# A second seven-product pair in the first FFN phase, the order of the high halves behind a late pair, and other PSUM banks behind a pair

## Chip, cores and metric

The kernel runs on one core of a Trainium2 chip. The metric is the device time of one execution in microseconds, the median over runs; lower is better. Weights start in HBM and are streamed through SBUF during the run.

## What is computed

A trunk of two layers over 256 tokens of width 1024. Each layer is a half-step SwiGLU FFN, a mixer (differential attention on four heads beside mLSTM on four heads), and a second half-step FFN, each between RMS norms:

```python
def _swiglu(h, w_in, w_out):
    gate, up = jnp.split(h @ w_in, 2, axis=-1)        # w_in 1024 x 5632, so 2816 hidden units
    return (jax.nn.silu(gate) * up) @ w_out           # w_out 2816 x 1024

for l in range(DEPTH):                                # DEPTH = 2
    g = norm_gains[l]
    h = _swiglu(_rmsnorm(x, g[0]), ffn_w_in[l, 0], ffn_w_out[l, 0])
    x = x + 0.5 * _rmsnorm(h, g[1])
    h = _mixer(_rmsnorm(x, g[2]), mix_w_in[l], mix_w_out[l], ...)
    x = x + _rmsnorm(h, g[3])
    h = _swiglu(_rmsnorm(x, g[4]), ffn_w_in[l, 1], ffn_w_out[l, 1])
    x = x + 0.5 * _rmsnorm(h, g[5])
```

The change touches the FFN phases alone. There are six phases: 0 FFN, 1 mixer, 2 FFN, 3 FFN, 4 mixer, 5 FFN.

## The kernel before, in words

**Splitting.** Every float32 operand is used as a high half (a copy rounded to fp32r, made by ScalarE) and a low half (the difference, made by VectorE), and every product is three matmuls: high by high, high by low, low by high (`mm3`, L507 to L509). A weight piece is 128 x 2048 float32, 1 MB, brought by one DMA that SyncE issues (`fetch`, L289) into one of three `wr` buffers or, each fourth time in an FFN, the `wx` buffer. `halved` splits each half of a piece: ScalarE writes `wh` (L296), VectorE writes `wl` (L297). Seven `wl`/`wh` pairs exist, and of every ten halves three are lent buffers of another pool (`k4`), by a counter that runs through all phases.

**An FFN phase.** The 2816 hidden units are eleven chunks of 256. An ordinary chunk takes two pieces of `w_in` and runs 48 matmuls of 128 x 512 (two token tiles t, two halves kh of the width, four k, three matmuls) into two PSUM banks, one for each t; then Silu on ScalarE, the product with `up` on VectorE, and a turn of the hidden values by DMA: `ffn_planes` (ScalarE copy into two 16-bit planes, L646, and a DMA transpose on SyncE's queue, L648), `ffn_joined` (ScalarE puts the planes together again, L654), `ffn_split`/`ffn_hilo` (high half on ScalarE, L670; low half on VectorE, L671). The output product of a chunk (`out_part`, step O) is 24 matmuls into four `bk` banks that accumulate over all chunks.

**A pair.** A step P computes two chunks at once as a 2 x 2 block product with seven instead of eight block products (Winograd's form): `pair` runs seven times twelve matmuls (`product`, L756) into banks b1, b2 (`pin`) and b3, b4 (`ptr`), 84 where two ordinary chunks take 96. For this the four weight blocks are added in `pair_blocks` (eight VectorE operations of 128 x 1024, L323) and split as seven operands (fourteen halves, where two chunks have eight), and the token blocks in `pair_tokens` (steps S). The banks are evacuated by L770 to L793; the two token tiles are sent to be turned as they are ready, tile 0 first (`h0`), then tile 1 (`v`).

**The order of work.** `ONE` lists the steps of phase 0 and `TWO` those of phases 2, 3 and 5: I an ordinary chunk, L the weight piece of an output product, O an output product, S and P as above. `ONE` has one pair (chunks 7 and 8), `TWO` has two (4, 5 and 8, 9). The last chunk, 10, is computed transposed (`in_turned`, L731 and L736). At the end the output products of the chunks in `END` (8, 9, 10) run first for tile 0, then for tile 1. A planner of the framework decides, when the program is built, in which order each engine gets its instructions, from its own estimates; TensorE alone follows the written order from "ending" to the end of an FFN, through a following mixer, and until "running" of the next FFN. On the chip each engine takes its instructions in the order set.

**Banks.** Two banks `pin`, two `ptr`, four `bk`. Ordinary chunks in the step list take two `ptr`, then two `pin`, by turns (`swap`, which a pair leaves alone). Chunk 3 before the first pair of `TWO` uses `pin`, and chunk 6 behind it `ptr`.

**Late pairs.** `pair_ready` joins both tiles of a pair and then splits: join t0, join t1, then the high and low halves of chunk c (t0, t1) and of chunk c + 1 (t0, t1). It runs in the I step behind the pair, for the pair (8, 9) behind the pieces of chunk 10.

Of the kernel before, what the change touches and what calls it, by code (L numbers as in the profile page):

```python
# [28 lines left out]
NT = S // P  # L29
# [4 lines left out]
CH = P  # L34
EPS = 1e-6
BIG = -1.0e30
ONE = "I2 L1 S0 O0 I3 L2 S1 O1 I4 L3 S2 O2 I5 L4 O3 I6 L5 O4 P7 L6 O5 L7 O6 I9 L8 O7 I10 L9".split()
TWO = "I2 L1 S0 O0 I3 L2 S1 O1 S2 P4 L3 O2 L4 O3 I6 L5 O4 I7 L6 O5 P8 L7 O6 L8 O7 I10 L9".split()
END = (8, 9, 10)
AHEAD = 2  # L40
AT = (0, 2, 6, 6, 9, 22, 24, 24, 26, 26, 36, 40, 30, 46, 34, 50, 46, 52, 52, 57, 61, 60, 61, 67, 67, 69, 71, 78, 74, 74, 80, 84)
# [19 lines left out]
def _pack(inp):  # L61


    f32 = np.float32
    x = np.asarray(inp["x"])
    w_in, w_out = np.asarray(inp["ffn_w_in"]), np.asarray(inp["ffn_w_out"])
    m_in, m_out = np.asarray(inp["mix_w_in"]), np.asarray(inp["mix_w_out"])
    g = np.asarray(inp["norm_gains"])
    w = np.empty((L * PIECES_LAYER, P, 2048), f32)

    def ffn(at, l, f):
        n = w_in[l, f].reshape(2, 4, P, 2, NC_FF, 256).transpose(0, 3, 2, 1, 4, 5)
        a = n.transpose(4, 0, 2, 3, 1, 5).reshape(NC_FF, 2, P, 2048)
        b = w_out[l, f].reshape(NC_FF, 2, P, D).transpose(0, 2, 1, 3).reshape(NC_FF, P, 2048)
        order = [a[0, 0], a[0, 1], a[1, 0], a[1, 1], b[0]]
        for step in TWO if l or f else ONE:
            c = int(step[1:])
            if step[0] == "P":
                order += [n[kh, g, :, :, c:c + 2].reshape(P, 2048) for kh, g in ((0, 0), (0, 1), (1, 1), (1, 0))]
            elif step[0] in "IL":  # L80
                order += [a[c, 0], a[c, 1]] if step[0] == "I" else [b[c]]
        for piece in order + [b[END[-1]]]:
            w[at] = piece
            at += 1

    for l in range(L):
        at = l * PIECES_LAYER
        ffn(at, l, 0)
        at += PIECES_FFN
        for n, lo in enumerate(MIX_GROUPS):  # L90
            a = m_in[l][:, lo:lo + 512].reshape(2, 4, P, 512).transpose(0, 2, 1, 3)
            w[at + 2 * n:at + 2 * n + 2] = a.reshape(2, P, 2048)
        at += 2 * len(MIX_GROUPS)
        w[at:at + 4] = m_out[l].reshape(4, 2, P, D).transpose(0, 2, 1, 3).reshape(4, P, 2048)
        ffn(at + 4, l, 1)
    for i in range(2):
        w[i] = w[i].reshape(P, 4, 512).transpose(1, 0, 2).reshape(P, 2048)

    arrays = {
        "x": x.reshape(NT, P, 2, 512).transpose(0, 2, 1, 3),  # L100
        "w": w,
        "gpost": g[:, 1::2].reshape(L * 3, D),
        "lam": np.asarray(inp["da_lambda"]).reshape(L, 256),
    }
    arrays = {k: np.ascontiguousarray(v) for k, v in arrays.items()}
    gpre = g[:, 0::2].reshape(L, 3, KT, P).transpose(3, 0, 1, 2).reshape(P, L * 3 * KT)
    arrays["c0"] = np.concatenate([np.eye(P, dtype=f32), gpre], 1)

    inv = (f32(10000.0) ** (-np.arange(0, 64, 2, dtype=f32) / f32(64))).astype(f32)
    ang = np.arange(S, dtype=f32)[:, None] * inv[None, :]  # L110
    cos, sin = np.cos(ang).astype(f32), np.sin(ang).astype(f32)
    rope = np.stack([np.concatenate([cos, cos], 1), np.concatenate([-sin, sin], 1)])
    s = np.arange(P)[:, None]
    j = np.arange(P)[None, :]
    mask = np.where((s // CH == j // CH) & (s <= j), 0.0, BIG).astype(f32)
    first = (np.arange(S) % CH == 0)
    scan = np.stack([np.where(first, 0.0, 1.0), np.where(first, BIG, 0.0)]).astype(f32)

    def everywhere(v):
        return np.broadcast_to(np.asarray(v).reshape(1, -1), (P, np.asarray(v).size))  # L120

    parts = {
        "wg": m_in[:, :, 3072:3080].reshape(L, KT, P, 8).transpose(2, 0, 1, 3),
        "rope": rope.reshape(2, NT, P, 64).transpose(2, 0, 1, 3),
        "convw": np.asarray(inp["ml_conv_w"]).reshape(L, 4, 4, P).transpose(3, 0, 2, 1),
        "convb": np.asarray(inp["ml_conv_b"]).reshape(L, 4, P).transpose(2, 0, 1),
        "gda": np.asarray(inp["da_subln_g"]).T,
        "gml": np.asarray(inp["ml_norm_g"]).T,
        "gateb": everywhere(inp["ml_gate_b"]),
    }  # L130
    arrays["c1"] = np.concatenate([parts[n].reshape(P, -1) for n, _ in C1], 1)
    arrays["mask"] = mask
    arrays["scan"] = np.ascontiguousarray(np.broadcast_to(scan.reshape(1, 512), (100, 512)))
    return arrays


class _Trunk:
# [521 lines left out]
    def ffn_split(self, hs):  # L659

        ops = [self.ffn_operand() for _ in range(NT)]
        for h, op in zip(hs, ops):
            self.ffn_hilo(h, *op)
        return [[tuple(v[:, k] for v in op) for k in range(2)] for op in ops]

    def ffn_operand(self):
# [40 lines left out]
    def ffn(self, pre, gi_post):  # L707
# [3 lines left out]
        def in_piece(t, kh, pin, w):  # L711
            xh, xl = xT[t][kh]
            for k in range(4):
                self.mm3(pin, xh[:, k, :], xl[:, k, :], *self.cols(w, k),
                         start=kh == 0 and k == 0, stop=kh == 1 and k == 3)

        def out_part(c, t, h, wo):
            for hf in range(2):
                for k in range(2):
                    self.mm3(po[t][hf], *h[t][k], *self.cols(wo, 2 * k + hf),  # L720
                             start=c == 0 and k == 0, stop=c == NC_FF - 1 and k == 1)
# [20 lines left out]
        def ready(c, others):  # L742
            if c in sent:
                hT = self.ffn_joined(sent.pop(c), others)
                hs[c] = self.ffn_split([hT[:, t] for t in range(NT)])

        def chunk(c, pins):
            h = self.t2("h", (P, NT, 256))
            i = [self.ffn_hidden(pins[t], r[t], h[:, t]) for t in range(NT)]
            send(c, h)  # L750
            ready(c - 1, i[:1])
# [44 lines left out]

        def pair_ready(others):
            c, turned = sent.pop("pair")
            hT = [self.ffn_joined(v, others) for v in turned]
            for j in range(2):  # L800
                hs[c + j] = self.ffn_split([h[:, j] for h in hT])

        hs, po, wo, sent = {}, [], {}, {}
        kept = bool(xT)
# [21 lines left out]
        else:  # L826
# [6 lines left out]
            h = self.t2("h", (P, NT, 256))  # L833
# [13 lines left out]
            h = self.t2("h", (P, NT, 256))  # L847
# [5 lines left out]
            ready(0, [i])  # L853
        both, swap = list(self.both), 0
        tokens = self.pair_tokens(both, kept)
        steps = TWO if kept else ONE
        for at, step in enumerate(steps):
            kind, c = step[0], int(step[1:])
            if kind == "P":
                pair(c)  # L860
            elif kind == "S":
                sums = next(tokens)
            elif kind == "L":
                if wo.get(c) is None:
                    wo[c] = self.piece()
            elif kind == "I":
                if c == 3:
                    g = self.load_gpost(gi_post)
                    yield "middle"
                ws = [self.piece()]  # L870
                cut = self.cut
                ws.append(self.piece())
                if "pair" in sent and c != END[-1]:
                    pair_ready([cut])
                for later in steps[at + 1:]:
                    if later[0] != "L":
                        break
                    wo[int(later[1:])] = self.piece()
                if c == END[-1]:
                    if "pair" in sent:  # L880
                        pair_ready([self.cut])
                    ready(c - 1, [self.cut])
                    break
                pins = [self.bank_pin() if swap else self.bank_tr() for _ in range(NT)]
                swap = 1 - swap
                for kh in range(2):
                    for t in range(NT):
                        in_piece(t, kh, pins[t], ws[kh])
                chunk(c, pins)
            else:  # L890
                if not po:
                    po = [[self.bank_bk() for _ in range(2)] for _ in range(NT)]
                for t in range(NT):
                    out_part(c, t, hs[c], wo[c])
# [574 lines left out]
```

## Time and profile before

| | us |
|---|---|
| median of 3 runs | 947.07 (947.05 to 948.33) |
| the profiled execution | 949.07, of it the span 947.3 |
| phase 0 (from the start to about 183) | TensorE busy 180.94 of 183.00 |
| TensorE busy in the span | 936.2 (99%), 4439 matmuls |
| VectorE, ScalarE busy | 757.5 (80%), 664.5 (70%) |

Busy shares are averages; the chain of work that ended last and the waits of TensorE say where time can be saved. A matmul's end in the trace is modelled, so distances between matmuls are taken from start to start.

### The profile page before, as it was taken

What the parts mean: (1) busy time and instruction counts of PE and PEld (TensorE: products, weight loads), DVE (VectorE), ACT (ScalarE), POOL (GpSimd) and SP (SyncE); (2) the same over time, 40 slices, a digit from 0 to 9 for tenths busy, and PEclk for the clock granted to TensorE, in tenths of its full rate; (3) what the DMA queues carried; (4) which work ended last, traced back from release to release, by engine and by line L of the source; (5) the groups of instructions that cost most, each with busy time, mean ns of one, the idle gap of its engine ahead of it and who ended that gap; (6) DMA issues with size and microseconds to landing.
All of it is one profiled execution on the core that took longest, in us unless ns stands there. A gap on an engine that the chain in (4) does not pass through costs nothing.

```text
span 947.3 us, 12104 instructions
## 1 busy us (share of the span) xinstructions
PE 936.2 (99%) x4439; PEld 772.3 (82%) x4439; DVE 757.5 (80%) x1062; ACT 664.5 (70%) x1028; POOL 28.3 (3%) x57
## 2 busy tenths in 40 slices
PE   9999999999999999999999999999999999999997
PEld 6888888888788888788788888888888888888885
DVE  7966885789767989699698887968898587996983
ACT  7966767577765877676577766866779476776872
POOL 2000000000010000000000000000000100000000
PEclk9999999999999999999999999999999999999999
DMA  9995476336372766747557576573464449477631
GB/s 341 344 305 158 147 268 206 134 134 213 120 266 90 286 180 249 195 138 296 166 189 256 164 278 191 189 245 122 175 215 139 173 142 288 132 282 189 217 128 45
DMA packets 69882, 189.34 MB, mean 200 GB/s; under 512 B 45274, under 2 KB 46426, under 8 KB 49086
## 3 DMA queue, kind: packets, MB, share of 16 engines
q1 hardware_dynamic: 69246, 187.95, 59.3%
q8 instruction: 35, 0.57, 0.2%
q10 hardware_dynamic: 576, 0.61, 0.2%
q14 instruction: 25, 0.20, 0.1%
HBM read 177.01 MB, written 1.05 MB: 188 GB/s over the span
## 4 chain that ended last, share of the span: by engine, by line
PE 97%; DMA 1%; ACT 1%; DVE 0%; issue 0%; SPq 0%; POOLq 0%; DVEq 0%; ACTq 0%
PE pin L507 11%; PE pin L509 11%; PE pin L508 11%; PE bk L507 10%; PE bk L509 10%; PE bk L508 10%; PE ptr L756 8%; PE pin L756 6%; PE ptr L507 4%; PE ptr L509 3%; PE ptr L508 3%; PE pin L731 2%; PE ptr L731 1%; PE ptr L533 1%; PE ptr L1091 1%; PE pin L736 1%
## 5 line engine op out<-in xcount | busy, mean ns | idle before, releaser
L297 DVE TENSOR_TENSOR wl<-wr,wh 128x1024 fp32r<-128x1024 f32 x262 | 313.1, 1222 | 62.6 <-ACT wh L296 60.3
L296 ACT ACTIVATE wh<-wr 128x1024 fp32r<-128x1024 f32 x262 | 268.8, 1052 | 58.0 <-PE pin L509 12.3
L507 PE MATMUL pin<-wh,both 128*128 128x512 f32 x448 | 177.0, 398 | 0.0
L509 PE MATMUL pin<-wh,both 128*128 128x512 f32 x448 | 174.7, 390 | 0.0
L508 PE MATMUL pin<-wl,both 128*128 128x512 f32 x448 | 174.6, 390 | 0.0
L508 PE MATMUL bk<-wl,hh 128*128 128x512 f32 x352 | 137.0, 389 | 0.0
L507 PE MATMUL bk<-wh,hh 128*128 128x512 f32 x352 | 134.9, 391 | 1.7 <-ACT hh L670 1.7
L509 PE MATMUL bk<-wh,hl 128*128 128x512 f32 x352 | 133.1, 389 | 0.0
L509 PEld LDWEIGHTS pin<-wh,both 128*128 128x128 f32 x448 | 84.1, 188 | 18.0
L507 PEld LDWEIGHTS pin<-wh,both 128*128 128x128 f32 x448 | 84.3, 188 | 17.5 <-issue 0.7
L508 PEld LDWEIGHTS pin<-wl,both 128*128 128x128 f32 x448 | 84.2, 188 | 16.2
L296 ACT ACTIVATE wh<-wx 128x1024 fp32r<-128x1024 f32 x62 | 64.4, 1053 | 31.3 <-DMA wx<-in_w_dram 11.6
L297 DVE TENSOR_TENSOR wl<-wx,wh 128x1024 fp32r<-128x1024 f32 x62 | 75.4, 1222 | 10.4 <-ACT wh L296 10.4
L507 PEld LDWEIGHTS bk<-wh,hh 128*128 128x128 f32 x352 | 66.1, 188 | 15.7 <-ACT hh L670 2.3
L509 PEld LDWEIGHTS bk<-wh,hl 128*128 128x128 f32 x352 | 66.1, 188 | 14.1 <-DVE hl L671 0.4
L508 PEld LDWEIGHTS bk<-wl,hh 128*128 128x128 f32 x352 | 66.1, 188 | 13.5
L756 PE MATMUL ptr<-wh,both 128*128 128x512 f32 x224 | 73.3, 389 | 0.0
L507 PE MATMUL ptr<-wh,both 128*128 128x512 f32 x144 | 55.0, 391 | 0.9 <-DVE h L785 0.9
L508 PE MATMUL ptr<-wl,both 128*128 128x512 f32 x144 | 55.7, 389 | 0.0
L509 PE MATMUL ptr<-wh,both 128*128 128x512 f32 x144 | 55.7, 389 | 0.0
L756 PE MATMUL pin<-wh,both 128*128 128x512 f32 x168 | 55.1, 389 | 0.0
L654 ACT ACTIVATE hT<-h 128x1024 uint16<-128x1024 uint16 x33 | 45.0, 1364 | 6.2 <-DMA h<-planes 5.9
(261 smaller groups left out, 1418.6 us busy)
## 6 DMA issues: line engine op xcount, KB each, us to landing
wr<-in_w_dram SPq DMA_DIRECT2D x131, 1024.0 KB, 4.9
wx<-in_w_dram SPq DMA_DIRECT2D x31, 1024.0 KB, 4.9
gpost<-in_gpost_dram SPq DMA_DIRECT2D x6, 512.0 KB, 6.1
wr<-in_w_dram SPq DMA_DIRECT2D x2, 512.0 KB, 7.3
wr<-in_w_dram SPq DMA_DIRECT2D x3, 256.0 KB, 5.6
x<-in_x_dram SPq DMA_DIRECT2D x3, 256.0 KB, 6.1
h<-planes SPq DMA_TRANSPOSE x33, 4.1
out_dram<-x SPq DMA_DIRECT2D x2, 256.0 KB, 2.1
```

Source lines behind the costliest of these rows:

```text
L296: ia = nc.scalar.activation(hi, raw, AF.Copy)
L297: iv = nc.vector.tensor_tensor(lo, raw, hi.bitcast(F32), op=ALU.subtract)
L507: mm(ps, xh, wh, start=start, stop=False)
L508: mm(ps, xh, wl, start=False, stop=False)
L509: mm(ps, xl, wh, start=False, stop=stop)
L533: nc.tensor.transpose(ptr[:, k, :], x[:, (4 * hf + k) * P:(4 * hf + k + 1) * P], self.ident)
L654: i = self.nc.scalar.activation(hT.rearrange("p a b n -> p (a b n)").bitcast(U16).rearrange("p (n u) -> p u n", u=2), turned.rearrange("p ...
L731: self.nc.tensor.matmul(b, self.cols(w[kh], k)[0][:, c], both[kh][:, k].rearrange("p i t -> p (i t)"), start=kh == 0 and k == 0, stop=Fals ...
L736: self.nc.tensor.matmul(b[:, 0:NT * P], self.cols(w[kh], k)[1][:, c], both[kh][:, k, 0:NT].rearrange("p i t -> p (i t)"), start=False, sto ...
L756: self.nc.tensor.matmul(b, st[:, k, :], self.cols(w, k)[mv], start=new and k == n == 0, stop=k == 3 and n == 2, skip_group_check=True)
L1091: self.T(ptr[:, b, :], a[:, b * P:(b + 1) * P], self.tr.ident)
```

## The change

Four edits. (1) Phase 0 follows the same list as the others, with pairs (4, 5) and (8, 9) in place of the one pair (7, 8); the order of the packed weight pieces follows. (2) `pair_ready` makes the four operands first and then goes tile by tile: join t0, high and low halves of t0 for both chunks, join t1 behind the two high halves of t0, high and low halves of t1. (3) After a pair `swap` is 1, so that the next ordinary chunk takes `pin` banks and the one after it `ptr`. (4) `ffn_split` gets its last line from a helper.

```diff
-ONE = "I2 L1 S0 O0 I3 L2 S1 O1 I4 L3 S2 O2 I5 L4 O3 I6 L5 O4 P7 L6 O5 L7 O6 I9 L8 O7 I10 L9".split()
-TWO = "I2 L1 S0 O0 I3 L2 S1 O1 S2 P4 L3 O2 L4 O3 I6 L5 O4 I7 L6 O5 P8 L7 O6 L8 O7 I10 L9".split()
+STEPS = "I2 L1 S0 O0 I3 L2 S1 O1 S2 P4 L3 O2 L4 O3 I6 L5 O4 I7 L6 O5 P8 L7 O6 L8 O7 I10 L9".split()
...
-        for step in TWO if l or f else ONE:
+        for step in STEPS:
...
             self.ffn_hilo(h, *op)
+        return self.ffn_pairs(ops)
+
+    @staticmethod
+    def ffn_pairs(ops):
         return [[tuple(v[:, k] for v in op) for k in range(2)] for op in ops]
...
             c, turned = sent.pop("pair")
-            hT = [self.ffn_joined(v, others) for v in turned]
+            ops = [[self.ffn_operand() for _ in range(NT)] for _ in range(2)]
+            for t in range(NT):
+                h = self.ffn_joined(turned[t], others)
+                others = [self.ffn_hilo(h[:, j], *ops[j][t])[0] for j in range(2)]
             for j in range(2):
-                hs[c + j] = self.ffn_split([h[:, j] for h in hT])
+                hs[c + j] = self.ffn_pairs(ops[j])
...
             if kind == "P":
                 pair(c)
+                swap = 1
```

More of the change, by code (lines that the diff above doesn't have):

```diff
@@ L855, in ffn @@
         tokens = self.pair_tokens(both, kept)
-        steps = TWO if kept else ONE
-        for at, step in enumerate(steps):
+        for at, step in enumerate(STEPS):
             kind, c = step[0], int(step[1:])
@@ L874, in ffn @@
                     pair_ready([cut])
-                for later in steps[at + 1:]:
+                for later in STEPS[at + 1:]:
                     if later[0] != "L":
```

## The prediction

> **What bounds the kernel now.** I read the head of the page first, then the chain of work that ended last, then TensorE's own waits, and went to the timeline only where a wait stands.
>
> ```profile
> span 947.3 us, 12104 instructions
> PE 936.2 (99%) x4439; PEld 772.3 (82%) x4439; DVE 757.5 (80%) x1062; ACT 664.5 (70%) x1028; POOL 28.3 (3%) x57
> PE 97%; DMA 1%; ACT 1%; DVE 0%; issue 0%; SPq 0%; POOLq 0%; DVEq 0%; ACTq 0%
> ```
>
> The span, the busy times, and the engines' shares of the chain: TensorE is busy 99% of the span and carries 97% of the chain. A matmul's modelled end overlaps the next start, so "busy" can hide short gaps. What a matmul costs comes from distances between starts; these two lines of the chain, in the pair of phase 0, show it:
>
> ```profile
> 112.44 2.72 PE pin L756 x12
> 115.16 2.72 PE ptr L756 x12
> ```
>
> Twelve 512-column matmuls take 2.72 us, 0.227 us each, group behind group. TensorE's waits (us in total, times, longest; the two rows left out are, like the second, from the first 10 us), and phase 0 behind its start:
>
> ```profile
> PE bk L507 <- ACT hh L670: 1.7, 1, 1.7
> PE ptr L455 <- DMA x<-in_x_dram: 0.9, 1, 0.9
> PE ptr L507 <- DVE h L785: 0.9, 3, 0.6
> ...
> ```
>
> ```profile
> 10.00:183.00 173.00, 173.00 (x784) 1.00 0.70 238
> ```
>
> The second row is the input at the start. The other two lie in FFN phases: 1.7 us once for a high half, 0.9 us in three places for an evacuation (L785). From 10 to 183 us TensorE has no gap. So time falls where matmuls go away or where one of these two waits goes away, and rises where a new wait appears.
>
> **The change, part by part.** The sum is made against the profiled execution: 949.07 us, span 947.3, so 1.77 us lie around the span. The median of the runs, 947.07, is 2.0 us below that execution; I subtract the sum from the median, since what is removed is matmuls and waits inside the span.
>
> *Phase 0's second pair: matmuls.* Before, chunks 4, 5, 9 are ordinary and 7, 8 a pair; after, 4, 5 and 8, 9 are pairs and 7 is ordinary. One more pair: 96 matmuls become 84. Twelve at 0.227 us: **-2.72 us**, all on the path, since this stretch has no gap. The Trainium skill, "TensorE: Matmul & The Clock Gate", section "Back-to-back issue gap", gives about 131 ns for a 512-column matmul in a sustained stream and about 216 ns for an isolated one; twelve would be worth 1.57 or 2.59 us, estimates from that page, and the sum below 4.81 or 5.83 us in place of 5.96. The trace's 2.72 us decides.
>
> *Phase 0's second pair: the other engines.* The durations:
>
> ```profile
> L297 DVE TENSOR_TENSOR wl<-wr,wh 128x1024 fp32r<-128x1024 f32 x262 | 313.1, 1222 | 62.6 <-ACT wh L296 60.3 <-PE bk L509 1.7
> L296 ACT ACTIVATE wh<-wr 128x1024 fp32r<-128x1024 f32 x262 | 268.8, 1052 | 58.0 <-PE pin L509 12.3 <-PE bk L509 11.5 <-DMA wr<-in_w_dram 9.3
> L323 DVE TENSOR_TENSOR qk<-qk,wr 128x1024 f32<-128x1024 f32 x14 | 17.1, 1222 | 0.1
> L785 DVE TENSOR_TENSOR h<-ptr,u 128x512 f32<-128x512 f32 x7 | 4.8, 686 | 2.8 <-PE ptr L756 2.8
> L793 DVE SCALAR_TENSOR_TENSOR v<-v,rs,u 128x512 f32<-128x512 f32 x7 | 5.2, 747 | 0.0
> L638 DVE SCALAR_TENSOR_TENSOR h<-pin,rs,sil 128x256 f32<-128x256 f32 x32 | 15.3, 481 | 0.9 <-ACT sil L268 0.9
> ```
>
> VectorE gets six more splits and eight block additions, 14 x 1.222 = 17.1 us, and the pair's evacuation (five operations of 0.69, two of 0.75, 4.9 us) for that of two chunks (4 x 0.48 = 1.9): +20.1 us. ScalarE gets six casts, 6 x 1.052 = 6.3 us; its Silus, planes and joins about balance. DMA bytes stay the same: four block pieces for four chunk pieces, one transpose for each tile instead of each chunk. They move on SyncE's queue, and the two diagonal-sum blocks hold `wr` buffers until their last addition, so the pieces behind (L4, chunk 6) are fetched later. POOL has no step here. The added token sums (S2) are not new, only written earlier. Whether this is covered is read from the stages; phase 3, which already has both pairs, is the model for phase 0 after:
>
> ```profile
> 0.00:183.00 183.00, 180.94 (x813) 147.88 (x814) 136.25 (x188) 130.11 (x188) 6.65 (x22) 1.00 0.71 240
> 483.00:650.00 167.00, 166.84 (x757) 138.47 (x755) 139.41 (x167) 120.43 (x155) 1.55 (x5) 1.00 0.64 213
> 40.00:63.00 23.00, 23.00 (x103) 19.06 (x102) 18.47 (x26) 19.18 (x28) 0.00 (x0) 1.00 0.99 323
> ```
>
> Phase 0 would hold (136.3 + 20.1) / 180 = 87% on VectorE and (130.1 + 6.3) / 180 = 76% on ScalarE, against 83% and 72% in phase 3, whose TensorE is busy 166.84 of 167.00 us. On average it fits. The critical place is the early one: the third row shows DMA at 0.99 share from 40 to 63 us, just before the new pair. So the question is VectorE's lead:
>
> ```profile
> 48.78 0.42 DVE L221 TENSOR_REDUCE c_lams<-lamp 128x4 f32<-128x256 f32 x1
> 50.88 2.36 DVE L297 TENSOR_TENSOR wl<-wr,wh 128x1024 fp32r<-128x1024 f32 x2 [1.68 <-PE bk L509]
> 53.08 1.06 ACT L296 ACTIVATE wh<-wx 128x1024 fp32r<-128x1024 f32 x1 [0.51 <-DMA wx<-in_w_dram]
> 63.32 0.39 PE L507 MATMUL ptr<-wh,both 128*128 128x512 f32 x1
> ...
> 514.87 1.23 DVE L323 TENSOR_TENSOR qk<-wx,wr 128x1024 f32<-128x1024 f32 x1 [0.31 <-DMA wr<-in_w_dram]
> 532.92 0.39 PE L756 MATMUL pin<-wh,both 128*128 128x512 f32 x1
> 553.07 4.63 DVE L297 TENSOR_TENSOR wl<-wr,wh 128x1024 fp32r<-128x1024 f32 x4
> ```
>
> Phase 3 begins the pair's additions at 514.87 and its first product at 532.92, a lead of 18.0 us. In phase 0 the work behind chunk 3 begins where O1 ends, at 63.32 (now chunk 4, then the pair). VectorE has caught up by then: it is done at 49.2 with all splits of L2 and waits at 50.88 for TensorE to free a weight half, so the halves are full. Of the 14.1 us until 63.3 it needs about 1.7 for the hidden values of chunks 2 and 3; lead about 12.4 us. The third block (`wx`) has landed by 53.08, the fourth one piece later, about 3.3 us at 323 GB/s, so 56.4. The need: 22 operations at 1.135 us (four back to back took 4.63 us, so (4.63 - 1.22) / 3 from one to the next) make 25.0 us, with four evacuations 27.4, against 19.0 us for 84 matmuls: a deficit of 8.4, with the first cast and split 10.7 us. 12.4 covers it, and O2 and O3 (48 matmuls, 10.9 us) stand ready as filling. I take **0**; bounds: 0, and -2.72 given back whole (the pair starves as long as it saves).
>
> *Banks behind a pair.* Three stalls, each the last matmul of an output product and the first of chunk 6 (phases 2, 3, 5):
>
> ```profile
> 382.68 0.39 PE L509 MATMUL bk<-wh,hl 128*128 128x512 f32 x1
> 383.68 0.47 PE L507 MATMUL ptr<-wh,both 128*128 128x512 f32 x1 [0.61 <-DVE h L785]
> ...
> 562.62 0.39 PE L509 MATMUL bk<-wh,hl 128*128 128x512 f32 x1
> 563.16 0.47 PE L507 MATMUL ptr<-wh,both 128*128 128x512 f32 x1 [0.16 <-DVE h L785]
> ...
> 849.86 0.39 PE L509 MATMUL bk<-wh,hl 128*128 128x512 f32 x1
> 850.41 0.47 PE L507 MATMUL ptr<-wh,both 128*128 128x512 f32 x1 [0.16 <-DVE h L785]
> ```
>
> Start to start 1.00, 0.54 and 0.55 us; less 0.227 that makes 0.77 + 0.32 + 0.32 = **1.41 us** (the waits row says 0.9, by modelled ends). Chunk 6 waits for a `ptr` bank, freed by L785 behind the pair's last products. With `pin` it takes b1 and b2, last read by the Silu of b1 and by L774, both long before. What is late next are chunk 6's weights:
>
> ```profile
> 381.70 1.23 DVE L297 TENSOR_TENSOR wl<-wr,wh 128x1024 fp32r<-128x1024 f32 x1 [1.72 <-ACT wh L296]
> 382.85 0.68 DVE L785 TENSOR_TENSOR h<-ptr,u 128x512 f32<-128x512 f32 x1
> ```
>
> The second half of its first piece is split at 381.70 to 382.93; it is needed six matmuls in, 382.91 + 1.36 = 384.27 us if chunk 6 starts without the gap. Margin 1.3 us, so nothing replaces the wait. Chunk 7 then takes `ptr`, a whole chunk (10.9 us) after the pair. In the late pair P5 writes b4, which chunk 7's tile 1 leaves; O5 (5.4 us) and P1 (2.7 us) lie between, against two operations of 0.5 us. Bounds: 1.41 gained, or 0 if the planner's new order puts another wait there. I take 1.41. Phase 0 had no such stall and gets none.
>
> *High halves behind each join.* The tail of phase 2 on ScalarE, then TensorE:
>
> ```profile
> 456.06 1.37 ACT L654 ACTIVATE hT<-h 128x1024 uint16<-128x1024 uint16 x1 [2.10 <-DMA h<-planes]
> 457.46 0.42 ACT L670 ACTIVATE hh<-hT 128x256 fp32r<-128x256 f32 x1
> 460.37 1.35 ACT L654 ACTIVATE hT<-v 128x1024 uint16<-128x1024 uint16 x1 [1.94 <-DMA v<-planes]
> 461.58 0.39 ACT L268 ACTIVATE su<-su 128x256 f32<-128x256 f32 x1
> 461.88 1.01 ACT L670 ACTIVATE hh<-hT 128x256 fp32r<-128x256 f32 x3
> ...
> 460.58 0.39 PE L509 MATMUL bk<-wh,hl 128*128 128x512 f32 x1
> 462.64 0.50 PE L507 MATMUL bk<-wh,hh 128*128 128x512 f32 x1 [1.67 <-ACT hh L670]
> ```
>
> Join t0 (456.06) gives one high half, 457.46; the next joins wait: ScalarE idles 1.94 us for the transpose of `v`, joins t1 at 460.37, and the three other high halves follow from 461.88. TensorE, which needs chunk 9 of tile 0 next, stands from 460.58 to 462.64: 2.06 - 0.227 = **1.83 us**. After, both halves of t0 are cast by 458.2, before 460.58 + 0.227, and t1 is needed only after 8 and 9 and 10 of tile 0 (36 matmuls, 8.2 us from 457.93, so 466.1), while its join ends at 461.7. Next late is chunk 10 of tile 0, needed at 457.93 + 24 x 0.227 = 463.4: its Silu stands at 461.58 behind the join, then product, cast and low half, about 463.3. That is close; bounds 1.83 gained, or 1.3 if it is half a microsecond late. I take 1.83. In phases 3 and 5 and, after, 0, the halves come before they are needed, so nothing. The rest of the edit (operands made earlier, a new order of ScalarE instructions) adds no instruction.
>
> Sum: 2.72 + 1.41 + 1.83 = **5.96 us**, so 947.07 - 5.96 = **941.1 us** (943.1 for an execution like the profiled one).
>
> **The rivals.** *The pair in phase 0 pays for itself.* For it: DMA at 0.99 share and 20.1 us more on an engine that was saturated until 49 us; buffers held longer. Against it: the lead above. Price: the 2.72 come back, the waits still go: 943.8.
>
> *The waits only move.* The planner orders anew, and a moved matmul meets another bank, weight half or low half. For it: chunk 10's margin of a tenth; against it: the 1.3 us at chunk 6. Only the matmuls remain: 944.3.
>
> *TensorE is not the limit.* If the modelled 99% hides that VectorE (80%) or the weight loads set the pace, neither matmuls nor waits count and the time stays at 947.1. Against it: groups of twelve at a constant 2.72 us, which a limit elsewhere would break. The Trainium skill, "Perfetto Trace Analysis", section "Identifying the Most-Contended Engine", speaks for this rival: matmul busy time is a poor measure, and weight-load busy time is to be read, here 82%, hardly above VectorE's 80%. The trace bears it out only in so far as four short gaps hid in "busy".
>
> *Slower.* One mechanism: VectorE enters the early pair of phase 0 without lead, and the planner has put O2 and O3 behind the pair instead of into it. Then TensorE waits up to the 10.7 us above less the lead. It decides for slower by over 0.2% (1.89 us) when the stall is over 5.96 + 1.89 = 7.85 us, so when the lead is under 2.9 us. With no lead: 951.8. Against it stand 12.4 us expected and 18.0 us in phase 3.
>
> **How the numbers follow.** Runs of this kernel spread over 1.3 us, so 0.2% (1.9 us) is about what a measurement can tell from no change. Chances: the forecast 0.62 (its own range 940.2 to 942.6, up by the chunk-10 margin and a stall of a microsecond in the new pair, down by what the runs spread), the pair that pays for itself 0.14, waits that move 0.10, TensorE not the limit 0.08, slower 0.06. Faster ends at 945.2: the first three but 0.03 of them, 0.83; same 0.11; slower 0.06. The range 940.2 to 945.0 takes in the forecast, the second and most of the third, 0.82.
>
> **What the profile of the changed kernel would show.** L756 at 672 matmuls (588 before), L507 to L509 96 fewer, and a second early pair in phase 0 from about 63 us, with TensorE without gaps to the end of the phase. If the pair starves, TensorE waits there for `wl` (L297) or for L323. The L785 row is gone from TensorE's waits, and chunk 6 writes `pin`. In phase 2's tail two high halves follow the first join without a gap, the wait of `bk` for `hh` is under 0.3 us, and ScalarE still idles for `v` with nobody waiting. The prediction is wrong if a new wait of over a microsecond stands at phase 0's pair, at chunk 6 or at chunk 10's output product.

## The result, and the profile after

The changed kernel takes 942.35 us (median of 5 runs, 942.2 to 944.36) against 948.01 us (5 runs on the same chip, the three of above among them): ratio 0.9946, 95% interval 0.9933 to 0.9960, so 5.1 us faster (3.8 to 6.4), 5.66 by the medians. The forecast was 941.1 from 947.07, 5.96 less; with five runs the kernel before lies 0.94 us higher than the 947.07 that the forecast started from, so the time came out 1.25 us above 941.1, while the change is 0.3 us smaller than forecast by the medians and 0.9 by the ratio. The profiled execution of the changed kernel took 944.36 us. The head of its page, then its pair groups beside those of before (TensorE, matmuls of a shape with their count; line numbers are each kernel's own, here and below):

```profile
span 942.6 us, 12085 instructions
PE 933.1 (99%) x4427; PEld 770.2 (82%) x4427; DVE 776.2 (82%) x1079; ACT 668.5 (71%) x1033; POOL 29.5 (3%) x57
PE 94%; DMA 2%; DVE 2%; ACT 2%; issue 0%; SPq 0%; POOL 0%; POOLq 0%; DVEq 0%; ACTq 0%
```

```profile
L759 PE MATMUL ptr<-wh,both 128*128 128x512 f32 x256 | 84.0, 389 | 0.0
L759 PE MATMUL pin<-wh,both 128*128 128x512 f32 x192 | 63.0, 389 | 0.0
```

```profile
L756 PE MATMUL ptr<-wh,both 128*128 128x512 f32 x224 | 73.3, 389 | 0.0
L756 PE MATMUL pin<-wh,both 128*128 128x512 f32 x168 | 55.1, 389 | 0.0
```

TensorE has 12 matmuls fewer and 8 pairs in place of 7 (256 : 224 and 192 : 168 are 8 : 7). It is still busy 99%, while its share of the chain fell from 97% to 94%, and VectorE and ScalarE now carry 2% each. What that costs is read from TensorE's own waits, here complete:

```profile
PE ptr L532 <- DVE x L589: 0.8, 2, 0.4
PE ptr L454 <- DMA x<-in_x_dram: 0.8, 1, 0.8
PE bk L495 <- PEq L1465: 0.8, 1, 0.8
PE bk L482 <- ACT wh L472: 0.4, 1, 0.4
PE bk L508 <- DVE hl L674: 0.2, 1, 0.2
```

Both waits on which the forecast rested are gone (`hh` L670, now L673; L785, now L788). In their place stand two lines that were not there: transposes (L532) waiting for x from the post-norm, and a high-by-low product waiting for `hl`, the low half of hidden values. Phase 0 from 10 us on, its whole, and the stretch beside the new pair (each row: stretch and length, busy time and instructions of TensorE, its weight loads, VectorE, ScalarE and GpSimd, then granted clock, busy share of the DMA engines, GB/s):

```profile
10.00:180.00 170.00, 170.00 (x772) 141.39 (x770) 149.53 (x194) 129.43 (x181) 3.13 (x8) 1.00 0.72 241
0.00:180.00 180.00, 178.06 (x801) 145.54 (x802) 153.29 (x205) 134.91 (x193) 6.57 (x22) 1.00 0.73 244
63.00:92.00 29.00, 29.00 (x130) 24.01 (x129) 27.59 (x29) 23.71 (x28) 0.00 (x0) 1.00 0.55 197
```

TensorE has no gap in phase 0 up to its end at 180 us. VectorE rose from 136.25 to 153.29 us there, by 17.0 (20.1 forecast). Where the 4.7 us between the two spans (947.3 and 942.6) lie, from start to start: 2.72 in matmuls, 1.41 + 1.83 in the two waits that went, against 0.55 us in phase 2's tail and 0.26 + 0.56 + 0.56 at the ends of phases 0, 2 and 3; the rest, 0.7 us, is in the first 12 us and in gaps of about 0.2 us and less. None of the new waits is over a microsecond, and none stands at phase 0's pair or at chunk 6, which writes `pin` now.

### The profile page after: what moved, and what is told of

Its sections match the earlier page's. It is cut to its first block, busy times and chain, and to the rows that moved or that the text cites. A ratio compares the mean times of both kernels' runs of the same rounds, so it can differ in the third digit from the quotient of the medians.

```text
span 942.6 us, 12085 instructions
## 1 busy us (share of the span) xinstructions
PE 933.1 (99%) x4427; PEld 770.2 (82%) x4427; DVE 776.2 (82%) x1079; ACT 668.5 (71%) x1033; POOL 29.5 (3%) x57
## 4 chain that ended last, share of the span: by engine, by line
PE 94%; DMA 2%; DVE 2%; ACT 2%; issue 0%; SPq 0%; POOL 0%; POOLq 0%; DVEq 0%; ACTq 0%
PE pin L506 11%; PE pin L508 10%; PE pin L507 10%; PE bk L506 9%; PE bk L507 9%; PE bk L508 9%; PE ptr L759 9%; PE pin L759 7%; PE ptr L507 3%; PE ptr L508 3%; PE ptr L506 3%; PE ptr L734 1%; PE pin L734 1%; PE ptr L532 1%; DMA v<-planes 1%; PE ptr L1097 1%
## 5 line engine op out<-in xcount | busy, mean ns | idle before, releaser
L506 PE MATMUL pin<-wh,both 128*128 128x512 f32 x432 | 171.2, 399 | 0.0
L507 PE MATMUL pin<-wl,both 128*128 128x512 f32 x432 | 168.4, 390 | 0.0
L508 PE MATMUL pin<-wh,both 128*128 128x512 f32 x432 | 168.2, 390 | 0.0
L508 PEld LDWEIGHTS pin<-wh,both 128*128 128x128 f32 x432 | 81.1, 188 | 17.4
L506 PEld LDWEIGHTS pin<-wh,both 128*128 128x128 f32 x432 | 81.3, 188 | 17.1 <-issue 0.7
L507 PEld LDWEIGHTS pin<-wl,both 128*128 128x128 f32 x432 | 81.2, 188 | 15.5
L759 PE MATMUL ptr<-wh,both 128*128 128x512 f32 x256 | 84.0, 389 | 0.0
L296 DVE TENSOR_TENSOR wl<-wx,wh 128x1024 fp32r<-128x1024 f32 x62 | 74.7, 1219 | 10.1 <-ACT wh L295 9.3
L759 PE MATMUL pin<-wh,both 128*128 128x512 f32 x192 | 63.0, 389 | 0.0
L759 PEld LDWEIGHTS ptr<-wh,both 128*128 128x128 f32 x256 | 48.1, 188 | 10.0
L507 PE MATMUL ptr<-wl,both 128*128 128x512 f32 x128 | 49.8, 389 | 0.0
L508 PE MATMUL ptr<-wh,both 128*128 128x512 f32 x128 | 49.8, 389 | 0.0
L759 PE MATMUL ptr<-wl,both 128*128 128x512 f32 x128 | 49.8, 389 | 0.0
```

The lines of the kernel that those rows point to most:

```text
L296: iv = nc.vector.tensor_tensor(lo, raw, hi.bitcast(F32), op=ALU.subtract)
L506: mm(ps, xh, wh, start=start, stop=False)
L507: mm(ps, xh, wl, start=False, stop=False)
L508: mm(ps, xl, wh, start=False, stop=stop)
L759: self.nc.tensor.matmul(b, st[:, k, :], self.cols(w, k)[mv], start=new and k == n == 0, stop=k == 3 and n == 2, skip_group_check=True)
```

## The experiments

The kernels ran in three groups of four, each group on another chip together with the kernel before, so ratios to before are compared across groups, not microseconds. "Old count" means the count of lent halves as it stands before the change at phase 1; phase 0's second pair makes six more halves, so the list shifts it by six. The traces show what such a shift does. Behind phase 0 every engine has the same order of instructions in the kernel before and in e9_list_count, and again the same in e1_list and e11_count; between these two groups the order differs in every engine but GpSimd. Which halves lie in lent buffers shifts along with the order, and no run here separates the two.

| kernel | edit | ratio to before (95%) | us |
|---|---|---|---|
| e1_list | list alone (count shifted) | 0.9949 (0.9935 to 0.9964) | -4.8 |
| e2_banks | banks alone | 0.9979 (0.9967 to 0.9992) | -2.0 |
| e3_joins | joins alone | 0.9973 (0.9963 to 0.9984) | -2.6 |
| e4_fourth | changed kernel, fourth half behind the post-norm | 0.9915 (0.9902 to 0.9928) | -8.1 |
| e9_list_count | list alone, old count | 0.9967 (0.9955 to 0.9979) | -3.1 |
| e10_after_count | changed kernel, old count | 0.9928 (0.9911 to 0.9946) | -6.8 |
| e6_adds2 | changed kernel, 8 more VectorE operations | 1.0002 (0.9989 to 1.0014) | +0.2 |
| e7_adds3 | changed kernel, 16 more | 1.0106 (1.0085 to 1.0127) | +10.1 |
| e11_count | shifted count alone | 0.9961 (0.9949 to 0.9974) | -3.7 |
| e12_best | changed kernel, old count, fourth half | 0.9917 (0.9898 to 0.9935) | -7.9 |
| e13_list_fourth | list and fourth half | 0.9919 (0.9898 to 0.9941) | -7.7 |
| after_again | changed kernel | 0.9936 (0.9918 to 0.9954) | -6.1 |

**One part at a time.** The list alone is the first two hunks of the diff; the banks alone are `swap = 1`; the joins alone are the new `pair_ready`.

> The kernel before with phase 0 on the list of the other phases, and nothing else. Theory (the terms add): L756 at 672, twelve matmuls fewer, -2.72 us; the old banks leave chunk 6 of phase 0 a wait on L785 as in phases 3 and 5, +0.3 to +0.8; so -1.9 to -2.4 us against before, and no other wait in phase 0. Rival (the pair pays for itself): waits of 2 us or more for split weights in phase 0, time within 0.7 us of before. On the new waits at the phase ends (TensorE on L589, 0.26 + 0.56 + 0.56 us after the change): if the list brings them (a shifted count of lent halves), they stand here too, and the gain is 0.5 to 1.0; if the order of the joins brings them, there is none.

> The kernel before with swap = 1 behind a pair, and nothing else. Theory: the three waits of chunk 6 on L785 (0.77 + 0.32 + 0.32 us) go and nothing takes their place: -1.4 us in the trace, the wait of 1.8 us in phase 2's tail stays. Rival (waits only move): another wait of 0.3 us or more at chunk 6 or 7, or at a phase end, and the trace within 0.5 us of before.

> The kernel before with the high halves behind each join, and nothing else. Theory: the 1.83 us in phase 2's tail become about 0.5 (chunk 10's low half comes late), so -1.3 us there. If the new order of ScalarE at the tail is what lets the planner put a fourth cast of the next phase ahead of the post-norm's square, the waits on L589 stand here (up to 0.26 + 0.56 + 0.56), and the net is about 0; if not, -1.3 us net.

TensorE's waits of the three (without the start), first the list, then the banks, then the joins:

```profile
PE ptr L533 <- DVE x L590: 0.6, 2, 0.5
PE bk L507 <- ACT hh L670: 0.3, 1, 0.3
```

```profile
PE bk L507 <- ACT hh L670: 1.2, 1, 1.2
```

```profile
PE ptr L507 <- DVE h L785: 0.9, 3, 0.6
```

Banks and joins did what the forecast says: with the banks alone L785 is gone, with the joins alone the wait for `hh` is gone, and neither brings a wait at a phase end. (With the banks alone the wait for `hh` stands, 1.2 us.) By their runs they are worth 2.0 (0.8 to 3.1) and 2.6 us (1.5 to 3.5), forecast 1.41 and 1.83. The list alone surprised: 4.8 us where 1.9 to 2.4 was expected, with **no wait on L785 in any phase** though the banks were the old ones, 0.3 us left for `hh`, and the new waits at the phase ends. Why L785 stopped mattering is seen on TensorE's timeline around the end of phase 3's first pair, the last matmul of the pair and the first of chunk 6, before and with the list alone, with VectorE's L785 of the latter (start, length, instruction, and in brackets the idle time before it with what ended it):

```profile
561.03 0.39 PE L756 MATMUL ptr<-wh,both 128*128 128x512 f32 x1
563.16 0.47 PE L507 MATMUL ptr<-wh,both 128*128 128x512 f32 x1 [0.16 <-DVE h L785]
```

```profile
552.66 0.39 PE L756 MATMUL ptr<-wh,both 128*128 128x512 f32 x1
557.19 0.39 PE L507 MATMUL ptr<-wh,both 128*128 128x512 f32 x1
...
553.97 0.68 DVE L785 TENSOR_TENSOR h<-ptr,u 128x512 f32<-128x512 f32 x1
```

Before, 2.13 us and 7 output matmuls lie between the two; with the list alone 4.53 us and 19. The evacuation is done at 554.65, long before chunk 6 asks for the bank at 557.19. Phase 3's code was not touched: the planner ordered it anew, and more output products stand between the pair and chunk 6.

**Is it the shifted count?** Two kernels complete the square: the list with the count put back, and the count shifted without the list.

```diff
-            seen = 0
+            seen, self.halves = 0, self.halves + 4 * (ph == 1)   # e9, e10, e12: old count (six back, modulo ten)
+            seen, self.halves = 0, self.halves + 6 * (ph == 1)   # e11: shifted count, list of before
```

> The kernel before with phase 0 on the list of the other phases and the count of lent halves put back at phase 1, so that from the end of phase 0 every engine has the same order of instructions as in the kernel before. Theory (the pair is worth its matmuls; what the list alone brought beyond them comes from the shifted count): TensorE's waits on L785 (0.77 + 0.32 + 0.32) and the 1.8 us in phase 2's tail stand again, no wait on L589, and the time is 2.7 us under before. Rival (the list itself removes those waits): they stay away and the time is 5 to 6 us under before, as with the list alone.

> The kernel before, phase 0 untouched, with six added to the count of lent halves at phase 1; from there every engine has the order of instructions that it has with the list alone. Theory (the shifted count, by the order that the planner then makes, removes the waits): no wait on L785, under 1 us left in phase 2's tail, new waits of 0.3 to 0.6 us on L589 at two or three phase ends; 1.5 to 2.8 us under before. Rival (phase 0's pair is needed for it): the waits of before stand, time as before.

TensorE's waits behind the start, first list with old count, then shifted count alone:

```profile
PE bk L507 <- ACT hh L670: 2.5, 2, 1.7
PE ptr L507 <- DVE h L785: 0.9, 3, 0.6
PE ptr L533 <- DVE x L590: 0.4, 1, 0.4
```

```profile
PE ptr L533 <- DVE x L590: 0.2, 1, 0.2
```

The count carries it. With the old count everything behind phase 0 has the order of before, both waits stand again (the one for `hh` even longer, 2.5 us in two places of phase 2's tail), and the pair is worth 3.1 us (2.0 to 4.3) against 2.72 forecast. With the count alone, and not one instruction less, both waits are gone and 3.7 us (2.5 to 4.8) are gained, more than the 1.5 to 2.8 expected, with short waits at the phase ends (0.31, 0.28 and 0.29 us from start to start).

> The changed kernel with the count of lent halves put back at phase 1. Theory (the terms of the sum hold at the old count, and the waits at the phase ends come from the shifted count): no wait on L785, none of over 0.1 us on L589, 0 to 0.6 us left in phase 2's tail: 0.8 to 1.4 us under the changed kernel, 5.4 to 6.0 us under before. Rival (the waits at the phase ends come from the order of the joins or from the banks): 0.5 us each on L589 stay, time as the changed kernel.

With the old count the whole change gives 6.8 us (5.1 to 8.4), with waits of 0.3 us for `hh` and none on x behind the start: the three terms of the forecast hold together there (5.96). Against the changed kernel it is not clearly faster, since the intervals overlap; the waits at the phase ends are gone as expected, though.

**The waits at the phase ends.** At the end of phase 3 ScalarE casts halves of the next phase's first weights and then squares for the post-norm of tile 0; x is written by VectorE behind that, and the next phase's transposes need x. ScalarE before, after, and with the fourth half ordered behind the post-norm; then TensorE after:

```profile
643.13 2.94 ACT L296 ACTIVATE wh<-wr 128x1024 fp32r<-128x1024 f32 x3
645.98 0.58 ACT L577 ACTIVATE junk<-bk 128x512 bf16<-128x512 f32 x1
```

```profile
638.28 3.89 ACT L295 ACTIVATE wh<-wr 128x1024 fp32r<-128x1024 f32 x4
642.07 0.57 ACT L576 ACTIVATE junk<-bk 128x512 bf16<-128x512 f32 x1
```

```profile
635.60 2.94 ACT L295 ACTIVATE wh<-wr 128x1024 fp32r<-128x1024 f32 x3
638.45 0.57 ACT L576 ACTIVATE junk<-bk 128x512 bf16<-128x512 f32 x1
...
639.59 1.05 ACT L295 ACTIVATE wh<-wr 128x1024 fp32r<-128x1024 f32 x1
```

```profile
646.61 0.41 PE L532 MATMUL ptr<-c,x 128*128 128x128 f32 x2 [0.40 <-DVE x L589]
```

After the change a fourth cast of 1.0 us stands ahead of the square: 3.89 us for four where three took 2.94. x is written 0.5 us later against the 24 matmuls of tile 1 that cover it, and TensorE waits. Before, that chain had no margin either: the transposes started 0.30 us behind the last matmul of tile 1, which is 0.07 us more than the usual 0.23, and 0.25 us more were lost among them until the second half of x was written. With the order of before, the list with the old count shows a wait of 0.4 us there.

```diff
-            self.turns = [self.guards] * 4 + [last[:1], post] if ph else []
+            self.turns = [self.guards] * 3 + [first, last[:1], post] if ph else []   # first: post-norm of tile 0
```

> The changed kernel, with the fourth half of the next phase's first weights ordered behind the post-norm of token tile 0 (its cast behind the second square on ScalarE, its split behind the write of x on VectorE) instead of behind the last chunk's high half. Theory (the new waits at the phase ends come from a fourth cast of 1.05 us ahead of the square): TensorE's waits on L589 go or fall under 0.1 us each, -1.1 to -1.4 us against the changed kernel, so about 941.1. Rival (the post-norm's own chain, from the last matmul of tile 0 through square, power and x, is longer than the 24 matmuls of tile 1 that cover it): the waits stay at 0.5 us.

All waits on x went, and the wait for `hl` with them: the fastest kernel here, 940.39 us, 8.1 us under before (6.8 to 9.3). The interval lies clear of the changed kernel's in the first comparison (3.8 to 6.4) and overlaps that of its second, below (4.4 to 7.8): that the fourth half's place brings something is shown by the waits, its size (some 2 to 3 us) only roughly. From start to start its trace has lost the two gaps of phase 2's tail, the three at the phase ends and three of 0.25 us inside the transposes, 2.7 us together.

> The changed kernel with the old count and with the fourth half of the next phase's weights behind the post-norm of tile 0. Theory: with the old count only 0.5 us in phase 2's tail and three gaps of 0.2 us inside the transposes at the phase ends (L532 behind L532) are left to take; the ordered fourth half took those three away in its own run: 0.4 to 0.8 us under the changed kernel with the old count. Rival: nothing left to gain, 942.

> The list alone, with the fourth half behind the post-norm of tile 0, and neither the banks nor the joins. Theory (at the shifted count the banks and the joins have nothing left to remove): as the changed kernel with the fourth half in place, within 0.8 us. Rival (the banks and joins carry the forecast's 3.2 us): 2 to 3 us slower than that.

> The changed kernel once more, beside the three others: 5.1 to 5.7 us under before, waits on L589 of 0.3 + 0.5 + 0.5 us, 0.3 to 0.6 us in phase 2's tail, and 1.5 to 2.2 us over the version with the fourth half in place.

The old count adds nothing to the ordered fourth half (ratio 0.9917 beside 0.9915). Beside the changed kernel with the old count (0.9928), the expectation holds in the trace: the three gaps inside the transposes are gone, and 0.6 us stay in phase 2's tail. In time it is not shown, since the intervals overlap. The changed kernel, once more, came out at 6.1 us (4.4 to 7.8) by the ratio, 5.4 by the medians; its waits at the phase ends were 0.26 + 0.23 + 0.88 us, so their sum came back (1.37 against 1.38), not the size of each, and it lies 1.9 us above e12 by the medians, as expected. The list and the fourth half alone do as well (0.9919), as expected at the shifted count, but not as safely: five of its runs took 939.6 to 941.5 us and the profiled one 945.14. That one shows what the joins guard against, in phase 2's tail (TensorE's wait, then ScalarE, then TensorE's busy time, matmuls and granted clock in two stretches):

```profile
PE bk L507 <- ACT hh L671: 2.0, 1, 2.0
```

```profile
456.04 1.34 ACT L655 ACTIVATE hT<-v 128x1024 uint16<-128x1024 uint16 x1 [2.58 <-DMA v<-planes]
457.50 0.71 ACT L671 ACTIVATE hh<-hT 128x256 fp32r<-128x256 f32 x2
```

```profile
455.56:458.97 3.41, 1.41 (x6) 1.00 0.00 0
458.97:462.38 3.41, 3.29 (x9) 0.50 0.00 0
```

The transpose of `v` landed late, ScalarE stood 2.58 us before the join of t1 with a high half of t0 behind it, and TensorE waited 2.0 us and then ran 3.41 us at half its clock. With the joins in place beside the fourth half, the runs lie within 1.3 us (e4_fourth 939.85 to 941.08, e12_best 940.57 to 941.84). Leaving aside e6 and e7, below, each kernel with the joins spread over 0.5 to 2.3 us and each without them over 2.0 to 5.6. The former have 4 to 7 runs and the latter 5 to 21, so that the joins narrow the spread is likely, but not shown.

**How much room has phase 0's early pair?** Each block addition is followed by one or two more VectorE operations on the same block, each block with itself, in that pair only; no other phase changes its order.

```diff
+                for _ in range(times - 1):          # times = 2 (e6) or 3 (e7) for chunk 4 of phase 0, else 1
+                    self.nc.vector.tensor_tensor(out[j], out[j], out[j], op=ALU.max)
```

> The changed kernel with each of the eight block additions of phase 0's first pair followed by one more VectorE operation of the same size on the same block (8 more of 1.13 us from one to the next, 9.1 us); all other phases keep their order. Theory (VectorE's lead of 9.8 us before the pair and the output products inside it cover the pair with room): TensorE waits 0 to 2 us more in phase 0. Rival (the new pair just fits, VectorE being busy 27.6 of 29 us beside it): 7 us or more of waits, time 7 us over the changed kernel.

> The same with two more operations behind each addition (16 more, 18.2 us). Theory: the cover is used up; of the second 9.1 us most is seen, waits of 5 to 10 us in phase 0. Rival (no room at all): 16 us or more. If nothing is seen here either, VectorE does not bound this stage.

TensorE's waits in phase 0 with 8 and with 16 more operations, and all engines in and behind the long wait with 8:

```profile
PE ptr L761 <- DVE v L783: 2.9, 1, 2.9
PE pin L761 <- DVE wl L296: 1.0, 2, 0.6
```

```profile
PE bk L508 <- ACT wh L295: 4.9, 1, 4.9
PE pin L761 <- ACT wh L295: 3.5, 1, 3.5
```

```profile
84.00:87.00 3.00, 0.11 (x1) 0.11 (x1) 3.00 (x6) 2.89 (x4) 0.00 (x0) 0.97 1.03 382
87.00:90.00 3.00, 3.00 (x7) 2.37 (x8) 3.00 (x3) 0.43 (x1) 0.00 (x0) 0.50 0.51 208
```

With 8 more operations the theory and its rival both missed: 9.1 us more of VectorE cost 5.3 us (1.0002 less 0.9946). The next 9.1 us cost 9.9, most of it seen, as expected, with 8.9 us in the waits; but the whole, 15.2 us, is close to what the rival said. These costs are not VectorE's delay alone. From start to start TensorE's gaps in phase 0 come to 4.4 us with 8 and 10.7 with 16 more operations, and the slow matmuls at half the clock behind the long gaps add 1.6 and 4.5 us. So of the first 9.1 us some 4.7 were covered; the second 9.1 brought 6.2 us of gaps and 2.9 us of lost clock. The pair has about 4.7 us of room, not 9.

## Why the prediction was right, and where it was not

*Matmuls of the second pair*: right. 3.1 us (2.0 to 4.3) by e9 against 2.72, and phase 0 without a gap.

*Its cover*: right in kind, too generous in size. The work for the pair begins at 50.73 us and the pair at 63.16:

```profile
50.73 2.36 DVE L296 TENSOR_TENSOR wl<-wr,wh 128x1024 fp32r<-128x1024 f32 x2 [1.68 <-PE bk L508]
53.34 1.22 DVE L322 TENSOR_TENSOR qk<-wr,wr 128x1024 f32<-128x1024 f32 x1
63.16 0.39 PE L759 MATMUL ptr<-wh,both 128*128 128x512 f32 x1
```

That is the 12.4 us of lead forecast, counted from the first split. The 18.0 us of phase 3 beside which the forecast set it were counted from the first addition; counted so, phase 0 has 9.8 (53.34 to 63.16). Of O2 and O3, 42 of 48 matmuls stand inside the pair, as said. With them as filling the forecast's numbers leave 12.4 + 10.9 - 10.7 = 12.6 us, but e6 shows some 4.7; where the rest went no run shows. The slower rival was not tried as it stands, since output products stayed inside the pair in e6 too. For 9.1 us less lead its sum gives a stall of 7.4 us; the run cost 5.3 and came out level with before.

*Banks*: right at the old count (e2, and L785 back in e9). But in the changed kernel the shifted count had already removed that wait, so the 1.41 us are not the banks' there: the list alone (4.8 us) and the whole change (5.1 and 6.1) do not differ beyond their intervals. The step that failed is "nothing replaces the wait", argued from the order of before, while the list moves a count that runs through all phases and the planner orders all of them anew. The text before the prediction names that count; the prediction gave it no term, and alone it is worth 3.7 us (e11), more than any term of the sum.

*High halves*: right that they remove the wait (e3). In the changed kernel most of that wait would have gone without them too: from start to start phase 2's tail has gaps of 0.47 + 0.29 us in the list alone, and none over 0.12 us with the shifted count alone. The margin of a tenth for chunk 10 did not hold in the changed kernel. ScalarE, then TensorE, in phase 2's tail:

```profile
450.87 1.37 ACT L653 ACTIVATE hT<-h 128x1024 uint16<-128x1024 uint16 x1 [0.57 <-DMA h<-planes]
452.27 0.72 ACT L673 ACTIVATE hh<-hT 128x256 fp32r<-128x256 f32 x2
457.33 1.37 ACT L653 ACTIVATE hT<-v 128x1024 uint16<-128x1024 uint16 x1 [2.85 <-DMA v<-planes]
459.74 0.30 ACT L673 ACTIVATE hh<-su 128x128 fp32r<-128x128 f32 x1
460.75 0.71 ACT L673 ACTIVATE hh<-su 128x128 fp32r<-128x128 f32 x3 [0.71 <-DVE su L697]
```

```profile
460.97 0.50 PE L508 MATMUL bk<-wh,hl 128*128 128x512 f32 x1 [0.15 <-DVE hl L674]
```

Two high halves follow the first join (452.27) and the join of t1 waits 2.85 us with none of t0 behind it, as forecast; but chunk 10's casts come at 459.74 and 460.75, and TensorE loses 0.24 + 0.32 us. That is the forecast's lower bound, 1.3 gained of 1.83.

*The rival "the waits only move"*: it came in part. 0.55 us in the tail and 1.38 at the phase ends are new, 1.9 of the 3.24 us removed; the forecast put its place at chunk 10 and chunk 6, and the larger part stood at the phase ends, which no step looked at.

*TensorE not the limit*: refuted; removing waits and matmuls moved the time by about what they measure (3.1 us for 2.72, 2.0 for 1.41, 2.6 for 1.83).

So the matmuls are right for the stated reason, but that the sum came within a microsecond is in part luck: the waits that the banks and joins remove were also removed by the order, and the new waits that the order brought, 1.9 us, happen to be about the size of what it gained besides. At the old count the sum holds for its own reasons (6.8 us, 5.1 to 8.4, against 5.96).

## What to carry to other kernels

Where a planner orders instructions from a state that runs through the program (a count of lent buffers here), an edit in one phase changes the order in all: compare the order of the untouched phases before putting a gain down to the edit, and hold the state fixed to see the edit alone. Of a wait that is to go, read too what stands with no margin next to it; here the post-norm at the phase ends was already 0.07 us late. Joining tile by tile may show little in the median and still keep a late transfer from mattering.

## What the hardware showed

TensorE's clock fell to half after less idling than I expected, and it did so in steps of 3.41 us. In the list with the fourth half the clock was 0.50 from 458.97 to 462.38 us, with matmuls 0.43 us apart instead of 0.227. With 8 more operations it was 0.50 from 86.84 to 90.25, again 3.41 us, and with 16 more twice for 6.83 us, two such stretches. The changes fit fixed steps: from 458.97 us to the clock's fall at the end of that run, 940.25, are 481.28 us, 141 times 3.413. Counted back in the same way from 942.54, where the clock falls at the end of the list with the old count, this is its stretch with the longest wait for `hh`, and the clock stayed at 1.00:

```profile
454.44:457.85 3.41, 1.71 (x10) 1.00 1.00 346
```

So TensorE busy for 1.71 of 3.41 us kept its clock, and busy for 1.41 it lost it. In the kernel before, the wait of 1.83 us falls on two stretches with 2.68 and 2.47 us busy, and the clock stayed too; whether the place of a wait decides beside its length, no run here shows. The Trainium skill, "TensorE: Matmul & The Clock Gate", section "What's actually happening", gives one idle window of about 3.4 us, free-running, as what halves the clock. The length agrees with the trace's 3.41 us, but the window did not have to be idle throughout: here 2.0 us of it were enough. By the slow matmuls, such a wait cost 1.6 us more than itself where the clock was low for 3.41 us (seven matmuls, in both runs), and 2.4 and 2.2 us where it was low for 6.83.
